# Query projection moved from token-by-token matmuls to the feature stage's block products, its RMS factor applied as the exponential's scale, sample attention in the third pass

## The chip, the core and the metric

The kernel runs on one core of a Trainium2 chip. The metric is the device time of one execution in microseconds (us); lower is better. The engines are called PE (TensorE, matmuls), DVE (VectorE), ACT (ScalarE), POOL (GpSimd) and SP (SyncE, which issues nearly all DMAs).

## The reference, cut to what matters

One layer for a prompt of 2048 tokens and 32 sample tokens (2080 together), model width 1024. The change touches the query path:

```python
h = rms_norm(x, norm_g) * (1.0 + scale[:, None, :]) + shift[:, None, :]
proj = h @ w_in
(q, k, v, za, qi, ki, wi, u, bg, cg, zb, ga, gb) = jnp.split(proj, ...)
q = partial_rope(rms_norm(q.reshape(B, T, 8, 128), q_norm_g), pos)   # 16 + 16 rotated dims of 128
k = partial_rope(rms_norm(k.reshape(B, T, 2, 128), k_norm_g), pos)
...
s = einsum('bqhgd,bqkhd->bqhgk', qg, kg) * (128 ** -0.5)
p = softmax(where(valid, s, -inf))                                   # over the 256 keys that an indexer picks
```

The RMS norm of a query is one factor for each token and head, times `q_norm_g` for each dimension. A rotation does not change the sum of squares, so the factor can be taken at any point before the softmax.

## The kernel before, in words

All large matmuls are fp32 split in two parts, so that a product is three matmuls (high by high, high by low, low by high). The program has four stages.

**Token stage** (`tok_steps`). The tokens come in two halves of 1040 columns (8 tiles of 128; the second half has a ninth tile of 32). `mk_h` transposes the normalised input, keeps it split in `hhi` and `hlo` and stores it in `h_d`. `chunk` then computes, for one tile of tokens and one piece of weights from the list `TOK`, 8 x 3 matmuls with tokens on the output's partitions (L759 to L761) into one of five accumulators `pm`. The pieces are `i0`, `i1` (indexer), `k`, `q0` to `q3` (256 columns each) and `v`. For `k` and `q` the norm's squares are ACT's (L726), the power is POOL's (L183), and scaling (L733) and rotation (L716 to L720) are DVE's; queries go to `q_d`, a row for each token. In the second half, `block_sums` (L670) forms differences of quarters of `h_d` for the next stage and stores them in `t_d`: 12 pieces, each of two loads of 352 (or 336) KB into the `x` buffers, of which there are four, four DVE operations and two stores. They are inserted among the last 50 steps, one for every three chunks.

**Feature stage** (`unit_steps`). The other projections are kept by feature: features on the output's partitions, tokens on the columns. They are computed by a scheme of seven half-size products in place of eight. A unit is two blocks of 128 features; each of its seven products is 12 matmuls for each of three chunks of 352, 352 and 336 columns (L991 to L993, in `mm`). `PASSES` deals the seven products over three passes: three, two and two. The first pass stores its results in `u_d`; the second ends the first half of the tokens, the third the second half (`fin`, which starts with an add of accumulator and stored part, L1053). `b_piece` loads and splits the token side of the products: from `h_d` or `t_d` to `ev` buffers (seven), ACT makes the high part `bh` and DVE the low part `bl` (L187). The first unit needs nine such pieces. There are 28 units in `PAIRS`.

Beside the units, `weave` mixes in the index selection of the blocks of queries (`index_steps`: scores by two matmuls each, L242 and L243, ReLU on ACT, accumulation on DVE, L246 and L248, then a bisection), nine blocks in the first pass, three in the second, three in the third. The attention of the 32 sample tokens (`sample_steps`) stands in the first pass, behind block 13.

**Attention** (`attention`). For each of 16 blocks of 128 queries, `prep` loads queries of a group of four heads, transposes them on PE (L1302) and splits them. `qk` computes scores (L1327 to L1329), adds a mask while it takes the row maximum (L1338), and applies `Exp` on ACT with the constant scale 128 ** -0.5 (L1342). `pv` multiplies with the values (L1363, L1371 to L1375).

**Output stage** (`outputs`): three more projections by the same scheme of seven products.

The order on each engine is set by a scheduler that places instructions by its own estimate of time, within the program's dependences; memory of a pool that has ended is given to the next one, so that the feature stage's `ev` buffers lie where the token stage's `x` buffers were, and its `wr` buffers where the token weights were.

## Time and profile before

| | |
|---|---|
| median of 3 runs | 2857.86 us (2855.92 to 2862.1) |
| profiled execution | 2855.3 us |
| its span, first to last instruction | 2853.4 us |
| PE busy | 2768.8 us, 97% |
| DVE / ACT / POOL busy | 2211.7 / 1486.7 / 971.3 us |
| token stage, last token matmul | starts at 460.96 us |
| first block product | starts at 465.63 us |
| first `u_d` load (second pass) | 1080.5 us |
| moved by DMA | 557.19 MB |

In the profile's lists a row of a group gives line, engine, operation, names and shape, the count, then busy time and mean duration, then the idle time of the engine just before them and what ended it. A row of time gives start, duration, engine, line, operation, and in brackets idle time before it. A row of waits gives who waited for whom, the sum, the number of times and the longest. "To landing" is the time from a DMA's issue to its last byte. A row of stretches gives busy time and number of instructions for each engine.

### The profile page before, as it was taken

The numbers are of one execution on the slowest core, as the hardware profiler recorded it, in microseconds if no ns is written. First come the engines' busy times: TensorE is split into PE (matmuls) and PEld (weight loads), VectorE is DVE, ScalarE is ACT, GpSimd is POOL, SyncE is SP. The second block draws the span as 40 slices with busy tenths as digits, with TensorE's granted clock in tenths as the row PEclk, the third lists the DMA queues.
The fourth block names the chain that finished last, engine by engine and source line by source line (L and its number), as shares of the span: only waits on it lengthen the run. The fifth ranks groups of instructions, "written<-read, shape, count | busy, mean of one in ns | idle before, by whom it ended". The sixth has DMA issues, their size and how long they took to land. (4 is left out here: it accounts for less than half of the span.)

```text
span 2853.4 us, 53721 instructions
## 1 busy us (share of the span) xinstructions
PE 2768.8 (97%) x18926; PEld 2674.1 (94%) x18926; DVE 2211.7 (78%) x4981; ACT 1486.7 (52%) x2861; POOL 971.3 (34%) x1440
## 2 busy tenths in 40 slices
PE   8999998999999999999999999999999999999998
PEld 6999998999999998999999999889999989999998
DVE  6666576767764778999998777878877768987988
ACT  4434334665545665655554433665655555454453
POOL 3324224545554532322323221576544430010100
PEclk9999999999999999999999999999999999999999
DMA  7425567544554546555576676576555359996785
GB/s 290 165 88 190 170 209 246 191 146 165 167 182 148 168 153 223 184 185 175 181 249 212 204 238 184 146 179 185 149 156 160 113 179 339 279 296 217 249 297 157
DMA packets 462097, 557.19 MB, mean 195 GB/s; under 512 B 171441, under 2 KB 353145, under 8 KB 460793
## 3 DMA queue, kind: packets, MB, share of 16 engines
q1 hardware_dynamic: 452952, 537.33, 59.1%
q0 software_dynamic: 4160, 12.06, 1.2%
q10 hardware_dynamic: 4704, 4.26, 0.4%
q8 instruction: 151, 2.47, 0.4%
q14 instruction: 130, 1.06, 0.1%
HBM read 369.17 MB, written 190.66 MB: 196 GB/s over the span
## 5 line engine op out<-in xcount | busy, mean ns | idle before, releaser
L991 PE MATMUL pm<-bh,wo 128*128 128x352 f32 (+1 forms) x2352 | 755.1, 323 | 6.5 <-ACT ev L1003 4.4
L992 PE MATMUL pm<-bl,wo 128*128 128x352 f32 (+1 forms) x2352 | 756.0, 322 | 0.0
L993 PE MATMUL pm<-bh,wo 128*128 128x352 f32 (+1 forms) x2352 | 754.2, 322 | 0.0
L991 PEld LDWEIGHTS pm<-bh,wo 128*128 128x128 f32 x2352 | 443.3, 189 | 15.1 <-ACT ev L1003 5.7
L992 PEld LDWEIGHTS pm<-bl,wo 128*128 128x128 f32 x2352 | 443.9, 189 | 4.8
L993 PEld LDWEIGHTS pm<-bh,wo 128*128 128x128 f32 x2352 | 442.3, 188 | 4.2 <-issue 0.2
L187 POOL TENSOR_TENSOR wo<-wr,wo 128x512 fp32r<-128x512 f32 x140 | 204.8, 1463 | 597.6 <-ACT wo L186 582.7
L759 PE MATMUL pm<-wh,hhi 128*128 128x256 f32 (+4 forms) x1088 | 307.9, 285 | 5.7 <-DVE sm L733 5.5
L760 PE MATMUL pm<-wl,hhi 128*128 128x256 f32 (+4 forms) x1088 | 307.2, 283 | 2.9 <-DVE wl L187 1.7
L761 PE MATMUL pm<-wh,hlo 128*128 128x256 f32 (+4 forms) x1088 | 305.0, 283 | 0.0
L248 DVE SCALAR_TENSOR_TENSOR sc<-pi,wi,sc 128x512 f32<-128x512 f32 (+3 forms) x287 | 192.2, 670 | 56.7 <-ACT pi L244 53.7
L186 ACT CAST th<-pt 128x512 fp32r<-128x512 f32 (+1 forms) x288 | 155.1, 561 | 137.7 <-PE pt L1363 131.1
L244 ACT ACTIVATE pi<-pi 128x512 f32<-128x512 f32 (+3 forms) x328 | 164.8, 516 | 113.1 <-PE pi L243 112.2
L1459 ACT CAST wh<-rw 128x1024 fp32r<-128x1024 f32 x128 | 134.3, 1052 | 166.0 <-PE ps L1634 81.2
L1633 PE MATMUL ps<-xh,wh 128*128 128x384 f32 (+1 forms) x672 | 214.2, 321 | 2.4 <-ACT wh L1459 0.9
L1634 PE MATMUL ps<-xl,wh 128*128 128x384 f32 (+1 forms) x672 | 214.4, 320 | 0.0
L187 DVE TENSOR_TENSOR tl<-pt,th 128x512 fp32r<-128x512 f32 (+1 forms) x288 | 183.9, 655 | 38.5 <-ACT th L186 37.3
L1635 PE MATMUL ps<-xh,wl 128*128 128x384 f32 (+1 forms) x672 | 211.7, 320 | 0.5 <-DVE wl L1460 0.5
L759 PEld LDWEIGHTS pm<-wh,hhi 128*128 128x128 f32 (+1 forms) x1088 | 198.9, 183 | 8.2 <-issue 3.5
L760 PEld LDWEIGHTS pm<-wl,hhi 128*128 128x128 f32 (+1 forms) x1088 | 199.2, 183 | 4.7 <-POOL wl L187 1.5
L761 PEld LDWEIGHTS pm<-wh,hlo 128*128 128x128 f32 (+1 forms) x1088 | 198.4, 183 | 1.0 <-DVE hlo L187 0.2
L1460 DVE TENSOR_TENSOR wl<-rw,wh 128x1024 fp32r<-128x1024 f32 x128 | 155.3, 1220 | 47.9 <-ACT wh L1459 47.7
(313 smaller groups left out, 7168.6 us busy)
## 6 DMA issues: line engine op xcount, KB each, us to landing
u<-u_d SPq DMA_DIRECT2D x112, 520.0 KB, 4.5
wr<-in_w_f_dram SPq DMA_DIRECT2D x84, 512.0 KB, 3.9
rw<-o_d SPq DMA_DIRECT2D x72, 512.0 KB, 6.8
u_d<-ev SPq DMA_DIRECT2D x168, 176.0 KB, 2.5
rw<-in_w_q_dram SPq DMA_DIRECT2D x56, 512.0 KB, 7.3
wr<-in_w_t_dram SPq DMA_DIRECT2D x32, 512.0 KB, 4.4
xa_d<-a SPq DMA_DIRECT2D x64, 256.0 KB, 3.1
s_d<-ws SPq DMA_DIRECT2D x56, 256.0 KB, 2.8
```

Of the source, the lines that this page charges most:

```text
L187: (eng or V).tensor_tensor(lo, src, hi.bitcast(F32), ALU.subtract)
L244: S.activation(pi[:n, :w], pi[:n, :w], AF.Relu)
L248: V.scalar_tensor_tensor(sc[:n, o:o + w], pi[:n, :w], wi[:n, b, h:h + 1], sc[:n, o:o + w], ALU.mult, ALU.add)
L759: T.matmul(pm[:n, :ncol], a, hi[:, kt, :ncol], start=(kt == 0), stop=False)
L760: T.matmul(pm[:n, :ncol], a, lo[:, kt, :ncol], start=False, stop=False)
L761: T.matmul(pm[:n, :ncol], b_, hi[:, kt, :ncol], start=False, stop=(kt == KT - 1))
L991: T.matmul(ps[:, :tb], wh[:, kt, :], bh[:, kt, :tb], start=(first and kt == 0), stop=False, **more)
L992: T.matmul(ps[:, :tb], wh[:, kt, :], bl[:, kt, :tb], start=False, stop=False, **more)
L993: T.matmul(ps[:, :tb], wl[:, kt, :], bh[:, kt, :tb], start=False, stop=(kt == 3), **more)
L1633: T.matmul(ps[:, :tb], wh[:, kt, wc], xh[:, kt, :tb], start=(first and kt == 0), stop=False, **more)
L1634: T.matmul(ps[:, :tb], wh[:, kt, wc], xl[:, kt, :tb], start=False, stop=False, **more)
L1635: T.matmul(ps[:, :tb], wl[:, kt, wc], xh[:, kt, :tb], start=False, stop=(kt == 3), **more)
```

## The change

- The query leaves `TOK` (four of eight pieces) and joins `PAIRS` as four units at the head of each pass, 32 units in all. Its weight columns are dealt (`QCOL`) so that a block of 128 features holds 16 dimensions of each of the eight heads; blocks 0 and 1 hold the 32 rotated dimensions.
- `query` takes the place of `fin` for these units: it adds the stored part, squares (ACT) and sums the squares over the eight blocks, multiplies with `q_norm_g`, rotates blocks 0 and 1 with tables that are loaded for it (two products on POOL, four operations on DVE for each chunk), and stores. A block of 128 features is stored by eight DMAs of 16 rows, so that `q_d` becomes [head, dimension, token].
- `factors` sums the squares over a head by ten small matmuls for each half, adds the epsilon and takes the power -0.5; the result, which holds the factor 128 ** -0.5 as well, goes to `r_d`, a row of 8 for each token.
- In attention the queries are loaded with the dimension on the partitions, so that their transposes go; the split reads the loaded tile. The factor of token and head is the scale of `Exp`, and of its bias. The sample attention likewise.
- The block sums of the second half start at step 15 of the token steps, one for every two chunks.
- The sample attention stands behind the third pass's index blocks.

Its core:

```diff
-PAIRS = []
+PAIRS = [("q", 2 * _u, 7 * KT + 2 * _u) for _u in range(KT // 2)]
-TOK += [(f"q{_i}", [(CQ + 256 * _i, 256)]) for _i in range(4)] + [("v", [(CV, 256)])]
+TOK += [("v", [(CV, 256)])]
+QCOL = [CQ + 128 * _h + 16 * _t + _i for _t in range(KT) for _h in range(8) for _i in range(16)]
...
-    q_d = dp.tile([NTOK, 1024], F32, name="q_d", tag="q_d")
+    q_d = dp.tile([8, P, NTOK], F32, name="q_d", tag="q_d")
+    r_d = dp.tile([NTOK, 8], F32, name="r_d", tag="r_d")
...
             def softmax():
-                V.tensor_scalar(w[:, 3:4], w[:, 2:3], -SCALE, None, ALU.mult)
-                S.activation(st["s"], st["s"], AF.Exp, bias=w[:, 3:4], scale=SCALE, accum_out=w[:, 4:5])
+                V.tensor_scalar(w[:, 3:4], w[:, 2:3], w[:, 6:7], -1.0, ALU.mult, ALU.mult)
+                S.activation(st["s"], st["s"], AF.Exp, bias=w[:, 3:4], scale=w[:, 6:7], accum_out=w[:, 4:5])
...
-                at = len(steps) - 50
+                at = 15
                 for j in range(12):
                     ch, kt = j // 4, j % 4
                     steps.insert(at, (0.0, lambda ch=ch, kt=kt: sums_load(ch, kt)))
                     steps.insert(at + 3, (0.1, lambda ch=ch, kt=kt: block_sums(ch, kt)))
-                    at += 5
+                    at += 4
...
+            if kind == "q":
+                query(ct, f, hf, ch, uu, ps, second)
+                return
...
+        def query(ct, f, hf, ch, uu, ps, second):
+            ...
+            V.tensor_tensor(u, u, ps[:, :tb], ALU.add)
+            ...
+            if ct == 0 and not second:
+                S.activation(sg, u, AF.Square)
+            else:
+                S.activation(sq, u, AF.Square)
+                V.tensor_tensor(sg, sg, sq, ALU.add)
+            S.mul(u, u, vecs[:, 88 + ct + f:89 + ct + f])
+            if ct == 0:
+                ...
+                G.tensor_tensor(x, a, sin, ALU.mult)
+                G.tensor_tensor(y, b, sin, ALU.mult)
+                V.tensor_tensor(a, a, cos, ALU.mult)
+                V.tensor_tensor(b, b, cos, ALU.mult)
+                V.tensor_tensor(a, a, y, ALU.subtract)
+                V.tensor_tensor(b, b, x, ALU.add)
+                if last:
+                    q_store(1 - f, t0, cvy["uu"])
+            if last:
+                q_store(ct + f, t0, uu)
+                if ct == KT - 2 and second:
+                    soon.append(lambda sg=cvy["ss"]: factors(sg, t0))
+        def q_store(t, t0, uu):
+            for h in range(8):
+                store(q_d[h, 16 * t:16 * t + 16, t0:t0 + HT], uu[16 * h:16 * h + 16, :HT])
+        def factors(sg, t0):
+            pq = pst.tile([P, 512], F32, name=nm("pq"), tag="pt")
+            for j in range(10):
+                T.matmul(pq[:104, 8 * j:8 * j + 8], sg[:, 104 * j:104 * j + 104], heads, start=True, stop=True)
+            ...
+            store(r_d[t0:t0 + HT, :].rearrange("(j p) h -> p j h", p=104), ss[:104].rearrange("p (j h) -> p j h", h=8))
...
             for b in blocks:
                 side += index_steps(env, b, False)
-                if b == 13:
-                    side += sample
+            if ps == 2:
+                side += sample
...
-                            load(q, q_d[r0:r0 + P, 512 * g:512 * g + 512])
+                            load(q.rearrange("p (h t) -> p h t", h=4), q_d[4 * g:4 * g + 4, :, r0:r0 + P].rearrange("h d t -> d h t"))
-                        pt = ptile().rearrange("p (h q) -> p h q", h=4)
-                        for h in range(4):
-                            T.transpose(pt[:, h, :], q[:, h * P:(h + 1) * P], ident)
-                        split(qh, ql, pt)
+                        split(qh, ql, q.rearrange("p (h q) -> p h q", h=4))
...
-                        V.tensor_scalar(sc[:, 16 + i:17 + i], sc[:, c1:c1 + 1], -SCALE, None, ALU.mult)
-                        S.activation(sm[:, :L], sm[:, :L], AF.Exp, bias=sc[:, 16 + i:17 + i], scale=SCALE, accum_out=sc[:, 18 + i:19 + i])
+                        r = st["r"][:, 2 * pr + i:2 * pr + i + 1]
+                        V.tensor_scalar(sc[:, 16 + i:17 + i], sc[:, c1:c1 + 1], r, -1.0, ALU.mult, ALU.mult)
+                        S.activation(sm[:, :L], sm[:, :L], AF.Exp, bias=sc[:, 16 + i:17 + i], scale=r, accum_out=sc[:, 18 + i:19 + i])
```

**How the order moves at the change from token to feature stage.** On PE, before, from the last token matmul on: `qd` to `pt` are transposes for the index scores of the sample block, `pi` index scores, `pm` with `bh` a block product.

```order
L761 MATMUL pm_6721<-wh_6153,hlo 32x256
L233 MATMUL pt_6989<-ident,qd_6983 128x32 x4
L242 MATMUL pi_6997<-kiS,qh_6987 32x352
L242 MATMUL pi_7007<-kiS,qh_6987 32x352
L991 MATMUL pm_6959<-bh_6775,wo_6771 128x352
```

Now, at the same place (line numbers are those of the changed kernel: L762 token, L237 transpose, L246 and L247 index score, L988 block product):

```order
L762 MATMUL pm_3856<-wh_3202,hlo 32x256
L237 MATMUL pt_4124<-ident,qd_4118 128x32 x4
L246 MATMUL pi_4132<-kiS,qh_4122 32x352
...
L237 MATMUL pt_4248<-ident,qd_4243 128x32 x4
L246 MATMUL pi_4274<-kiS,qh_4246 32x352
...
L237 MATMUL pt_4726<-ident,qd_4721 128x128 x4
L246 MATMUL pi_4734<-kiT,qh_4724 128x512
...
L247 MATMUL pi_4824<-kiT,ql_4725 128x512
L988 MATMUL pm_4094<-bh_3910,wo_3906 128x352
```

Between the last token matmul and the first block product stand now 48 index matmuls of 352 columns, 16 of 512 and 12 transposes, where two index matmuls and four transposes stood.

On SP, before, from the last block sum's load to the first operand of the feature stage (`x` and `t_d` the block sums, `q_d` the queries' stores, `ev` the operand):

```order
L661 DMA x_6115<-h_d 128x2x336
L776 DMA q_d<-sm_6143 128x256
L776 DMA q_d<-sm_6196 128x256
L672 DMA t_d<-x_6114 256x1x336
L776 DMA q_d<-sm_6243 128x256
L672 DMA t_d<-x_6115 256x1x336
L226 DMA qd_7108<-qi_d 32x4x64
...
L776 DMA q_d<-sm_6451 128x256
L977 DMA ev_6777<-h_d 128x352
```

Now (L662 and L673 the block sums, L925 feature weights, L974 the operand):

```order
L673 DMA t_d<-x_3647 256x1x336
L673 DMA t_d<-x_3648 256x1x336
L662 DMA x_3718<-h_d 128x2x336
L662 DMA x_3719<-h_d 128x2x336
L230 DMA qd_5710<-qi_d 128x4x64
L231 DMA qd_5710<-qi_d 128x4x64
L673 DMA t_d<-x_3718 256x1x336
L673 DMA t_d<-x_3719 256x1x336
L925 DMA wr_3902<-in_w_f_dram 128x1024
L925 DMA wr_3904<-in_w_f_dram 128x1024
L974 DMA ev_3912<-h_d 128x352
```

Of the 24 stores of the block sums, the last fourteen have no store of a token tile's keys between them any more; before, stores of queries stood between them to the end.

On DVE, after the last key tile's rotation (L721), what follows in the changed kernel (L671 the block sums, L209 an index key):

```order
L721 TENSOR_TENSOR sm_3591<-sm_3594 32x2x16
L209 TENSOR_TENSOR kiS<-pt_3606,kh_3608 64x128
L671 TENSOR_TENSOR x_3156<-x_3156 128x352
L671 TENSOR_TENSOR x_3156<-x_3157,x_3156 128x352
L671 TENSOR_TENSOR x_3157<-x_3157,x_3156 128x352
L671 TENSOR_TENSOR x_3157<-x_3157 128x352
L671 TENSOR_TENSOR x_3268<-x_3268 128x352
```

The piece that begins here is the sixth of twelve; before, the last piece was followed by the norm and rotation of six more query tiles. In the third pass, the sample attention's last matmul stands 144 block products ahead of attention's first score.

More of the change, by code (lines that the diff above doesn't have):

```diff
@@ L410, in prep @@
                     load(st["m"][h * NS:(h + 1) * NS, :], ms_d)
-                q = env.small()
-                load(q[:NS], q_d[SEQ:, 512 * g:512 * g + 512])
-                pt = env.pst.tile([P, 512], F32, name=nm("pt"), tag="pt")
+                load(st["q"].rearrange("p (h t) -> p h t", h=4), q_d[4 * g:4 * g + 4, :, SEQ:].rearrange("h d t -> d h t"))
+                w = st["w"] = env.ip.tile([P, 64], F32, name=nm("w"), tag="w", bufs=2)
                 for h in range(4):
-                    T.transpose(pt[:, h * NS:(h + 1) * NS], q[:NS, h * P:(h + 1) * P], ident[:NS, :NS])
-                S.copy(st["q"], pt[:, :P])
-                st["w"] = env.ip.tile([P, 64], F32, name=nm("w"), tag="w", bufs=2)
+                    load(w[h * NS:(h + 1) * NS, 6:7], r_d[SEQ:, 4 * g + h:4 * g + h + 1])
             def logits(c):
@@ L1396, in attention @@
                     qst = sp.tile([P, SEQ], F32, name=nm("s"), tag="low")[:, :1024]
-                    load(qst, q_d[order[0] * P:order[0] * P + P, :])
+                    load(qst.rearrange("p (h t) -> p h t", h=8), q_d[:, :, order[0] * P:order[0] * P + P].rearrange("h d t -> d h t"))
                     vst = ahead(v_d)
@@ L1821, in _consts @@
     table = np.concatenate([table, np.zeros((17 * P - NTOK, 48), np.float32)]).reshape(17, P, 48).transpose(1, 0, 2).reshape(P, 17 * 48)
-    return {"rope": table, "ident": np.eye(P, dtype=np.float32), "rows": rows}
+    turns = np.stack([np.tile(t.T, (8, 1)) for t in cols[:2]]).astype(np.float32)
+    heads = np.kron(np.eye(8), np.ones((16, 1)))
+    return {"rope": table, "turns": turns, "ident": np.concatenate([np.eye(P), heads], axis=1).astype(np.float32), "rows": rows}
 def _chunks(w):
-    cols = np.concatenate([np.asarray(w)[:, c:c + D] for c in FCOL], axis=1)
-    return cols.reshape(KT, P, 7 * KT, P).transpose(2, 1, 0, 3).reshape(7 * KT, P, KT * P)
+    cols = np.concatenate([np.asarray(w)[:, c:c + D] for c in FCOL] + [np.asarray(w)[:, QCOL]], axis=1)
+    return cols.reshape(KT, P, 8 * KT, P).transpose(2, 1, 0, 3).reshape(8 * KT, P, KT * P)
 def _wide(w):
```

66 lines of the change are left out of this document (48 added, 18 removed).

## The prediction

> **What bounds the kernel now.** I read the page's busy totals first, then the stretches of the span, then who waits for whom on TensorE. The totals say that one engine is nearly full:
>
> ```profile
> span 2853.4 us, 53721 instructions
> PE 2768.8 (97%) x18926; PEld 2674.1 (94%) x18926; DVE 2211.7 (78%) x4981; ACT 1486.7 (52%) x2861; POOL 971.3 (34%) x1440
> ```
>
> TensorE is idle for 2853.4 - 2768.8 = 85 us in all, so a change is worth what it takes from TensorE's stream, less any new hole in it. The stretches show both, and what stands behind TensorE in each stage (columns: length, then busy time and count by engine, granted clock, DMA share, GB/s):
>
> ```profile
> core 0: us, PE busy (x) PEld busy (x) DVE busy (x) ACT busy (x) POOL busy (x), PEclk, DMA share, GB/s
> 150.00:200.00 50.00, 50.00 (x444) 50.00 (x443) 32.09 (x158) 17.01 (x78) 13.70 (x20) 1.00 0.31 103
> 350.00:400.00 50.00, 46.89 (x406) 45.93 (x405) 37.26 (x161) 16.81 (x78) 13.30 (x21) 1.00 0.72 228
> 1250.00:1300.00 50.00, 49.51 (x306) 48.45 (x305) 48.87 (x105) 27.34 (x53) 14.13 (x18) 1.00 0.51 174
> 1400.00:1440.00 40.00, 40.00 (x254) 40.00 (x253) 35.35 (x83) 22.36 (x47) 11.87 (x13) 1.00 0.64 215
> 1800.00:1850.00 50.00, 46.76 (x333) 43.35 (x332) 39.68 (x133) 28.73 (x73) 33.37 (x98) 0.94 0.66 151
> 1900.00:1950.00 50.00, 44.51 (x311) 40.79 (x310) 36.09 (x94) 27.86 (x57) 33.60 (x87) 0.97 0.69 187
> 2350.00:2400.00 50.00, 47.97 (x272) 46.68 (x271) 39.51 (x61) 27.07 (x32) 7.42 (x14) 1.00 0.97 345
> ```
>
> At 150 the token stage runs without a hole: 444 matmuls of 256 columns, less one or two cut by the edges, in 50 us, so one starts every 0.113 us. At 1400 only block products run: 254 in 40 us, one every 0.1575 us for 352 or 336 columns. These spacings, not the durations of 0.28 and 0.32 us, are what a matmul costs, since the next starts before the last ends. At 350, in the second half of the tokens, DMA is 0.72 full at 228 GB/s, so full would be 317. At 1250, in the second pass, VectorE is as full as TensorE. At 1800 to 1950 attention's first blocks leave TensorE idle for some 3 to 5 us in 50.
>
> **The sum.** *Query projection out of the token stage.* Four pieces, 17 tiles, 8 contraction steps, 3 products: 1632 matmuls, x 0.113 = -184.4 us. *Four more units in the feature stage.* 7 products, 3 column chunks, 4 steps, 3 matmuls each: 1008 x 0.1575 = +158.8. Net -25.6. TensorE was full in both stretches, so this is path.
>
> On these two spacings the Trainium skill (TensorE: Matmul & The Clock Gate, Back-to-back issue gap) has a sustained roofline of 81 ns at 128 columns and 131 ns at 512. An estimate between those points is 98 and 109 ns, and the net would be -50 us; the rows are longer, by more at 350 columns, and they decide.
>
> *Attention's query transposes.* The list of TensorE in order of time, one group of four:
>
> ```profile
> 1789.58 0.28 PE L1372 MATMUL po<-tl,vhi 128*128 128x256 f32 x1
> 1789.70 0.29 PE L1373 MATMUL po<-th,vlo 128*128 128x256 f32 x1
> 1789.83 0.60 PE L1302 MATMUL pt<-ident,in 128*128 128x128 f32 x4
> 1790.18 0.36 PE L1371 MATMUL po<-th,vhi 128*128 128x256 f32 x1
> 1790.38 0.35 PE L1372 MATMUL po<-tl,vhi 128*128 128x256 f32 x1
> 1790.57 0.28 PE L1373 MATMUL po<-th,vlo 128*128 128x256 f32 x1
> 1790.69 0.28 PE L1371 MATMUL po<-th,vhi 128*128 128x256 f32 x1
> ```
>
> Four take 0.35 us and the next two start 0.20 and 0.19 apart where 0.12 is usual: 0.50 a group. 16 blocks have two: 32 x 0.50 = 16. Half of the blocks lie in the stretches at 1800 to 1950, where TensorE has holes that such a group may merely fill; I take -12, bounds -16 and 0. The split behind them stays, from SBUF instead of PSUM. The loads get runs of 512 bytes instead of 2 KB; before, they held TensorE for
>
> ```profile
> PE pt L1302 <- DMA in<-q_d: 2.5, 2, 1.3
> ```
>
> in all, and from now on the split waits for them, with TensorE's work on the block before as cover.
>
> *Waits that go with the norm.* TensorE's waits in the token stage are mostly for the norm that frees an accumulator:
>
> ```profile
> PE pm L759 <- DVE sm L733: 5.5, 6, 1.4
> ```
>
> Four of its five users go: -4, bounds -5.5 and 0. VectorE's own norm, rotation and weight splits for the queries go too; in that stage they lay beside TensorE.
>
> *The RMS factors.* Two groups of ten small matmuls, f32 as the transposes are: at a transpose's 0.35 / 4 about 0.9 us a group, or 1.25 with the slower matmuls after it: +2; bounds 0 and +4 if each group waits 1 us for VectorE's sum. The factor as scale replaces a constant and costs nothing; 16 small loads share SP with the mask loads.
>
> *The change of stage, and who is late next.* The block sums (L670) have to be done before the feature stage: their four `x` buffers lie where its `ev` buffers come. Before, their work and landings were:
>
> ```profile
> L670 DVE TENSOR_TENSOR x<-x x24: 487/510/526, 323.6 to 432.2; 128x352 f32<-128x352 f32 x16, 128x336 f32<-128x336 f32 x8
> DMA x<-h_d: 13.5, 12
> x<-h_d SPq DMA_DIRECT2D x16, 352.0 KB, 3.7
> t_d<-x SPq DMA_DIRECT2D x16, 352.0 KB, 2.7
> 405.88 0.61 SPq L661 DMA_DIRECT2D x<-h_d  x1
> L248 DVE SCALAR_TENSOR_TENSOR sc<-pi,wi,sc 128x512 f32<-128x512 f32 (+3 forms) x287 | 192.2, 670 | 56.7 <-ACT pi L244 53.7
> L186 ACT CAST bh<-ev 128x352 fp32r<-128x352 f32 (+1 forms) x84 | 37.4, 477 | 18.4 <-DMA ev<-h_d 12.3 <-DMA ev<-t_d 5.5 <-DVE y L1045 0.3
> ev<-h_d SPq DMA_DIRECT2D x8, 176.0 KB, 4.3
> ```
>
> Twelve pieces ran from 323.6 to 432.2, hidden under queries until 461. Now they must run beside the last 22 chunks of index, key and value, 22 x 24 x 0.113 = 60 us of TensorE. Two pieces fit in the buffers. A cycle is two loads to issue (1.2), 3.7 to land, four operations of 0.51, a store to issue (0.6), 2.7 to land, 1.1 of wait as in the 12 waits of the row, and, an estimate, 1.5 for VectorE's queue, two or three operations: 12.8 us for two pieces, 6.4 each. DMA gives no less: 16.6 MB of sums, 4.2 of keys and values, 1.9 of weights and index is 22.7 MB, 72 us at 317 GB/s, 6.0 a piece. I take 6.5: 78 us, then 4.3 for the first `ev`, 0.5 cast, 0.5 difference (as long as a block sum's), 1.2 to issue two: the first block product 84.5 us after the first load, 24.5 us behind the last token matmul. Index scores pulled into the hole (the order above) fill 48 x 0.16 + 16 x 0.24, by columns, and 12 transposes x 0.09: 12.6; VectorE needs about that gap for them anyway (32 scores of some 0.6, the row's mean for 512 columns being 0.67, and three pieces of 2.04 are 25 us). That leaves 12 idle. The nine operand pieces behind, 6.2 MB, want 19.6 us at 317 GB/s where TensorE wants 9 x 12 x 0.1575 = 17: 3 more. Before, the same place idled:
>
> ```profile
> 464.85 0.61 PE L242 MATMUL pi<-kiS,qh 128*32 128x352 f32 x2 [3.25 <-ACT qh L186]
> 465.63 0.66 PE L991 MATMUL pm<-bh,wo 128*128 128x352 f32 x1 [0.17 <-ACT wo L186]
> 477.14 0.34 PE L242 MATMUL pi<-kiS,qh 128*32 128x352 f32 x1 [2.65 <-DVE sc L248]
> 478.05 0.34 PE L242 MATMUL pi<-kiS,qh 128*32 128x352 f32 x1 [0.41 <-DVE sc L246]
> 478.73 0.50 PE L242 MATMUL pi<-kiS,qh 128*32 128x352 f32 x1 [0.17 <-DVE sc L248]
> ```
>
> 6.6 us. So +12 + 3 - 6.6, about +9.
>
> *Query units in passes two and three.* A unit lasts 6 x 12 x 0.1575 = 11.3 us without index work. VectorE's part per step is an add, and a square's add of the same size; rotation adds four operations per chunk in one unit:
>
> ```profile
> L1053 DVE TENSOR_TENSOR u<-u,pm 128x352 f32<-128x352 f32 (+1 forms) x240 | 121.0, 506 | 24.3 <-PE pm L993 23.5
> L940 POOL TENSOR_TENSOR ws<-wr 128x512 f32<-128x512 f32 x28 | 37.1, 1325 | 93.6 <-DMA wr<-in_w_f_dram 55.1 <-DMA u_d<-ev 19.0 <-issue 13.3
> u<-u_d SPq DMA_DIRECT2D x112, 520.0 KB, 4.5
> L1014 SPq DMA_DIRECT2D u<-u_d x112: 319/320/1540, 1080.5 to 1764.6; - x112
> ```
>
> Per pass 24 + 21 + 12 operations of 0.506 are 29 us in 45 us of TensorE time, less than VectorE's 48.87 of 50 around it: covered by TensorE. The rotation's subtraction waits for two products on POOL, 0.9 us each by columns, beside two of VectorE's own; behind it in VectorE's queue stand the adds that free accumulators, and five accumulators give 4 x 12 x 0.1575 = 7.6 us of slack. Instead of one store a tile there are eight of 16 rows; the sixteen at the end of the first unit hold back, on SP, the load of the third unit's `u` by about 16 x 0.32 = 5 us plus landing; the second unit's 11.3 us and the slack cover that and the load's 4.5: +2 for what they don't, bounds 0 and +29 if VectorE's part is not covered.
>
> *Sample attention* keeps its work, less eight transposes (under 1 us, left out). In the third pass it ends 144 block-product matmuls, 23 us, before attention's first scores: no term, and if that cover were gone, attention would wait for it by no more than one group's last steps.
>
> Sum: -25.6 - 12 - 4 + 2 + 9 + 2 = -28.6. The profiled execution took 2855.3 (span 2853.4 and 1.9 around it), so 2826.7; the median of the runs is 2857.86, 2.6 above it, so 2829.3 there.
>
> **Rivals.** *No hole at the change of stage.* With the shortest landings, 3.3 and 2.7, and no queueing, the cycle is 1.2 + 3.3 + 2.04 + 0.6 + 2.7 = 9.8, 4.9 a piece, 59 us, and the sums end with the tokens:
>
> ```profile
> DMA to landing us min/median/max: 3.3/3.7/6.1
> DMA to landing us min/median/max: 2.7/2.7/3.8
> ```
>
> Then the +9 goes, and with all 16 us of the transposes it is 2816. Against it: the loads of the whole stretch then ask for more than 317 GB/s. The Trainium skill (DMA: Bandwidth & Descriptors, Anatomy of one DMA) has about 2 us plus bytes over 436 GB/s, 2.8 us as an estimate for these loads, on this rival's side; the trace's 3.3 at best differs.
>
> *VectorE is the bound in the second pass.* At 48.87 of 50 it has no room if the index selection's operations crowd the new ones; each accumulator is then freed late, and 29 us come onto the path: 2858, no change. For it speaks that stretch, against it that the selection's total stays while the pass grows.
>
> *DMA holds the feature stage back, and it is slower.* Before, from 300 to 461, it moved
>
> ```profile
> DMA packets 26861, 33.34 MB, mean 207 GB/s; under 512 B 3231, under 2 KB 25690, under 8 KB 26842
> ```
>
> If 207 GB/s is what these short packets get, the 30 MB up to the ninth operand piece (22.7, 6.2 and 1 of weights) take 145 us against 60 + 17 of TensorE: 68 us late, less 12.6 filled and the 6.6 of before, +49 in place of +9: 2869. It decides below 224 GB/s, where the whole gain of 37.6 us outside this term is used up. Against it: 228 at a share of 0.72, and 345 in the stretch at 2350.
>
> **How the numbers follow.** Forecast 0.62, no hole 0.14, VectorE 0.13, DMA 0.11. The forecast's own terms reach from 2812 to 2843. The range 2810 to 2860 takes in the first three and leaves out the fourth and some of the tails. Within 0.2% (5.7 us, about what a measurement of this kernel can tell from no change) is 2852 to 2864: 0.13, mostly the third case. Slower: 0.09. Faster: 0.78.
>
> **What would show it.** The last token matmul starts near 273 (461 less 184 and 4); between it and the first block product lie 20 to 30 us with index scores in them; the block sums follow one another at 6 to 7 us; the feature stage is some 160 us longer; no waits for the query in attention, which is 10 to 16 us shorter. Wrong if the hole passes 50 us, or if the second pass has more than 5 us of new idle TensorE time.

## The result, and the profile after

The changed kernel takes 2874.12 us (median of 6 runs, 2868.78 to 2879.44), the kernel before 2857.7 on the same chip. The ratio is 1.0051, 95% interval 1.0029 to 1.0073: slower by 0.5%, where the forecast was 2829 and faster. Medians and ratios below are of undisturbed executions; two executions of the experiments' kernels, of 3538 and 15314 us, are left out as slow. The profiled execution took 2868.78 us, its span is 2867.0. From the page of the changed kernel, the busy totals:

```profile
span 2867.0 us, 51829 instructions
PE 2749.5 (96%) x18206; PEld 2642.5 (92%) x18206; DVE 2193.7 (77%) x4549; ACT 1508.4 (53%) x2719; POOL 1049.3 (37%) x1430
```

TensorE has 19 us less to do, and is idle for 2867.0 - 2749.5 = 117.5 us where it was 85. The stretches show where:

```profile
core 0: us, PE busy (x) PEld busy (x) DVE busy (x) ACT busy (x) POOL busy (x), PEclk, DMA share, GB/s
250.00:300.00 50.00, 33.81 (x230) 25.36 (x229) 24.72 (x61) 11.20 (x31) 2.29 (x6) 0.78 0.78 245
300.00:350.00 50.00, 34.26 (x121) 21.68 (x121) 46.32 (x87) 37.80 (x79) 25.85 (x21) 0.77 0.77 247
1000.00:1050.00 50.00, 44.20 (x245) 40.99 (x244) 41.40 (x94) 37.28 (x76) 18.56 (x18) 0.93 0.68 200
1250.00:1300.00 50.00, 50.00 (x318) 49.98 (x317) 34.63 (x58) 19.04 (x36) 13.17 (x9) 1.00 0.59 184
```

Between 250 and 350 TensorE ran 351 instructions; a full stretch of 50 us holds 318 of the feature stage's or 444 of the token stage's. The second pass (1250) is full, and VectorE has 15 us free in it. TensorE in order of time, at the change of stage:

```profile
270.99 0.28 PE L762 MATMUL pm<-wh,hlo 128*32 128x256 f32 x1
271.20 0.43 PE L237 MATMUL pt<-ident,qd 32*128 32x32 f32 x4
275.88 0.76 PE L246 MATMUL pi<-kiS,qh 128*32 128x352 f32 x2 [4.25 <-DVE kiS L209]
284.17 0.50 PE L247 MATMUL pi<-kiS,ql 128*32 128x352 f32 x1 [7.53 <-DVE ql L191]
...
318.41 0.32 PE L988 MATMUL pm<-bh,wo 128*128 128x352 f32 x1
320.15 0.66 PE L989 MATMUL pm<-bl,wo 128*128 128x352 f32 x1 [0.31 <-DVE bl L191]
```

The last token matmul starts at 270.99, the first block product at 318.4: 47.4 us apart, where it was 465.63 - 460.96 = 4.7. What VectorE and SP's queue do there (first row: duration, then first and last start; the others in order of time; last row of the group of loads):

```profile
L671 DVE TENSOR_TENSOR x<-x x24: 485/522/589, 213.8 to 308.9; 128x352 f32<-128x352 f32 x16, 128x336 f32<-128x336 f32 x8
269.98 1.74 SPq L662 DMA_DIRECT2D x<-h_d  x2
276.32 1.68 SPq L673 DMA_DIRECT2D t_d<-x  x2
278.04 1.30 SPq L662 DMA_DIRECT2D x<-h_d  x2
283.82 1.84 SPq L673 DMA_DIRECT2D t_d<-x  x2
285.71 1.28 SPq L662 DMA_DIRECT2D x<-h_d  x2
DMA to landing us min/median/max: 3.9/4.7/4.9
```

The block sums run from 213.8 to 308.9, and the loads of the twelve pieces start from 207.5 to 302.2: eleven steps of 8.6 us. SP issues the two stores of a piece, and only then the two loads of the next: one piece is in flight, and each cycle is an issue, a landing of 4.7 and VectorE's four sums in a row, with index scores between them on VectorE (stores waited 10.0 us in all behind those, by the list of SP's waits).

The length of attention comes from its first score and the first matmul of the output stage, the two rows of before and then the two of after:

```profile
L1327 PE MATMUL ps<-khi,qh x320: 277/394/796, 1780.4 to 2316.5; 128*128 128x512 f32 x92, 128*128 128x384 f32 x59, 128*128 128x256 f32 x5, 128*128 128x128 f32 x4
L1633 PE MATMUL ps<-xh,wh x672: 283/336/452, 2349.2 to 2790.7; 128*128 128x384 f32 x112, 128*128 128x272 f32 x56
```

```profile
L1392 PE MATMUL ps<-khi,qh x320: 222/394/657, 1808.6 to 2328.1; 128*128 128x512 f32 x91, 128*128 128x384 f32 x60, 128*128 128x256 f32 x5, 128*128 128x128 f32 x4
L1699 PE MATMUL ps<-xh,wh x672: 283/336/445, 2359.8 to 2803.9; 128*128 128x384 f32 x112, 128*128 128x272 f32 x56
```

| part, us | before | after | difference | forecast |
|---|---|---|---|---|
| up to the last token matmul | 461.0 | 271.0 | -190.0 | -188.4 |
| hole to the first block product | 4.7 | 47.4 | +42.7 | +19.8 (24.5 - 4.7) |
| first block product to first score | 1314.8 | 1490.2 | +175.4 | about +152 |
| first score to output stage | 568.8 | 551.2 | -17.6 | -12 |
| output stage | 504.2 | 507.2 | +3.0 | 0 |

The forecast's +152 is 158.8 of block products, +2 and +2 for factors and query units, +3 for operand pieces, less the 12.6 of index scores that the hole was to take out and 2 of idle time before. So two terms are wrong by some 23 us each: the hole, and the feature stage.

### The profile page after: what moved, and what is told of

It reads as the page before. It is cut to its first block, busy times and chain, and to the rows that moved or that the text cites. A ratio compares the mean times of both kernels' runs of the same rounds, so it can differ in the third digit from the quotient of the medians.

```text
span 2867.0 us, 51829 instructions
## 1 busy us (share of the span) xinstructions
PE 2749.5 (96%) x18206; PEld 2642.5 (92%) x18206; DVE 2193.7 (77%) x4549; ACT 1508.4 (53%) x2719; POOL 1049.3 (37%) x1430
## 5 line engine op out<-in xcount | busy, mean ns | idle before, releaser
L988 PE MATMUL pm<-bh,wo 128*128 128x352 f32 (+1 forms) x2688 | 867.0, 324 | 13.1 <-DVE u L1087 8.4
L989 PE MATMUL pm<-bl,wo 128*128 128x352 f32 (+1 forms) x2688 | 866.3, 322 | 2.2 <-DVE bl L191 2.1
L990 PE MATMUL pm<-bh,wo 128*128 128x352 f32 (+1 forms) x2688 | 864.0, 323 | 0.4 <-POOL wo L191 0.4
L988 PEld LDWEIGHTS pm<-bh,wo 128*128 128x128 f32 x2688 | 508.1, 189 | 21.6 <-DVE u L1087 10.1
L989 PEld LDWEIGHTS pm<-bl,wo 128*128 128x128 f32 x2688 | 509.2, 189 | 9.4 <-DVE bl L191 3.5
L990 PEld LDWEIGHTS pm<-bh,wo 128*128 128x128 f32 x2688 | 507.9, 189 | 4.0 <-POOL wo L191 0.8
L1408 ACT ACTIVATE s<-s,sc,rts 128x640 f32<-128x640 f32 (+15 forms) x128 | 166.0, 1298 | 49.6 <-DVE sc L1407 43.5
L1780 POOL DMA_DIRECT2D out_dram<-om x60 | 31.7, 534 | 389.9 <-DVE om L1778 389.9
L190 ACT CAST wo<-wr 128x512 fp32r<-128x512 f32 x160 | 98.3, 616 | 144.3 <-PE pm L989 114.4
L315 ACT ACTIVATE low<-sc,w 32x1056 f32<-32x1056 f32 (+14 forms) x105 | 136.6, 1301 | 62.7 <-DVE w L320 61.8
L1053 DVE TENSOR_TENSOR u<-u,pm 128x352 f32<-128x352 f32 (+1 forms) x240 | 122.2, 510 | 56.6 <-PE pm L990 54.9
L1437 PE MATMUL po<-th,vhi 128*128 128x256 f32 x544 | 158.9, 292 | 5.3 <-ACT th L190 3.0
```

The source lines that it names most:

```text
L190: S.copy(hi, src)
L988: T.matmul(ps[:, :tb], wh[:, kt, :], bh[:, kt, :tb], start=(first and kt == 0), stop=False, **more)
L989: T.matmul(ps[:, :tb], wh[:, kt, :], bl[:, kt, :tb], start=False, stop=False, **more)
L990: T.matmul(ps[:, :tb], wl[:, kt, :], bh[:, kt, :tb], start=False, stop=(kt == 3), **more)
L1408: S.activation(sm[:, :L], sm[:, :L], AF.Exp, bias=sc[:, 16 + i:17 + i], scale=r, accum_out=sc[:, 18 + i:19 + i])
```

## The experiments

Theory A: the hole is the chain of the block sums, one piece in flight because of the order on SP's queue. Theory B: the transfers themselves set it. Theory C: the feature stage's start is slow by itself, since VectorE is crowded. Theory D: the eight stores of a query tile hold passes two and three back. Twelve kernels; ratios are to the kernel before, in the same set of runs:

| kernel | median us | ratio, 95% interval | hole us | first block product to first score |
|---|---|---|---|---|
| loads one piece ahead | 2864.54 | 1.0021 (1.0007 to 1.0035) | 21.9 | 1504.6 |
| no block sums | 2827.98 | 0.9901 (0.9880 to 0.9923) | 4.7 | 1491.6 |
| index woven in later | 2875.66 | 1.0067 (1.0046 to 1.0089) | 47.2 | 1492.7 |
| sums started earlier | 2851.53 | 0.9981 (0.9968 to 0.9993) | 11.0 | 1498.1 |
| earlier and ahead | 2850.72 | 0.9960 (0.9942 to 0.9977) | 11.3 | 1498.1 |
| one store a query tile | 2876.71 | 1.0055 (1.0041 to 1.0070) | 49.4 | 1491.8 |
| index held back | 2884.58 | 1.0097 (1.0072 to 1.0121) | 42.3 | 1507.9 |
| earlier, ahead, one store | 2850.08 | 0.9963 (0.9951 to 0.9976) | 7.2 | 1496.6 |
| plain query units | 2865.72 | 1.0020 (1.0009 to 1.0031) | 49.3 | 1480.4 |
| constant scale in Exp | 2873.42 | 1.0057 (1.0041 to 1.0072) | 47.7 | 1494.6 |
| square sums on POOL | 2849.06 | 0.9968 (0.9955 to 0.9980) | 8.9 | 1496.1 |
| half of the splits on POOL | 2850.50 | 0.9979 (0.9966 to 0.9991) | 10.3 | 1495.9 |

**Loads one piece ahead.**

```diff
+                steps.insert(at, (0.0, lambda: sums_load(0, 0)))
                 for j in range(12):
-                    steps.insert(at, (0.0, lambda ch=ch, kt=kt: sums_load(ch, kt)))
-                    steps.insert(at + 3, (0.1, lambda ch=ch, kt=kt: block_sums(ch, kt)))
+                    if j < 11:
+                        steps.insert(at + 1, (0.0, lambda j=j: sums_load((j + 1) // 4, (j + 1) % 4)))
+                    steps.insert(at + 3, (0.1, lambda j=j: block_sums(j // 4, j % 4)))
```

> The changed kernel with the loads of each block-sum piece issued before the sums of the piece before it, so that two pieces are in flight; nothing else is different. Theory A (queue order: in the changed kernel the loads of a piece stand on SP's queue behind the stores of the piece before, so only one piece is in flight and pieces follow each other every 8.3 to 8.6 us): the pieces come 6.4 to 7 us apart, the last sum ends near 290 instead of 309, the first block product starts near 300 instead of 318, and the time falls by 12 to 20 us, to 2854 to 2862. Theory B (the transfers set the pace, at 170 to 297 GB/s in that stretch): the pieces stay over 8 us apart and the time stays within 4 us of 2874.

Its sums, its first block product, and two of its stretches:

```profile
L671 DVE TENSOR_TENSOR x<-x x24: 485/522/536, 212.6 to 288.3; 128x352 f32<-128x352 f32 x16, 128x336 f32<-128x336 f32 x8
L989 PE MATMUL pm<-bh,wo x2688: 311/321/726, 296.5 to 1799.8; 128*128 128x352 f32 x132, 128*128 128x336 f32 x60
```

```profile
250.00:260.00 10.00, 10.00 (x89) 10.00 (x89) 7.79 (x39) 1.30 (x7) 2.38 (x5) 1.00 0.98 308
260.00:270.00 10.00, 10.00 (x90) 10.00 (x89) 3.61 (x7) 1.56 (x5) 0.42 (x2) 1.00 1.02 330
```

The loads of a piece now follow those of the piece before by 6.3 us (209.1 to 278.4 in eleven steps), the last sum starts at 288.3, the hole is 21.9: A, and near what the forecast had taken for the change itself (6.5 and 24.5). B does not explain the 8.6 us, but it is the next limit: in these 20 us DMA is full, at 308 to 330 GB/s. Only some 9 us of the 25 from the hole reach the end, where 12 to 20 were expected: the token stage ends 3.7 us later and the feature stage is 14 longer. Less index work was done in the hole (48 instructions of TensorE for 77) and the first unit is still slow (21 products of a line in its first 42 us); how the 14 divide between the two was not measured.

**No block sums** (the sums are left out, and eleven of twelve pieces of their loads; the stores of all twelve stay).

```diff
+            if (ch, kt) != (0, 0):
+                return
...
-                tc.keep_in_program_order(V.tensor_tensor(o, p, q, ALU.subtract))
+            x1, x2 = halved[0, 0]
```

> The changed kernel with the block sums left out: the two buffers of the first piece are loaded once and stored for all twelve pieces, so the twelve stores to the DRAM array stay, and eleven of twelve pieces of loads and all of VectorE's subtractions go (the outputs of the feature stage are then not the reference's). Theory A (the chain of load, subtraction and store sets the hole of 47.5 us): the first block product comes 5 to 15 us behind the last token matmul and the time falls by 30 to 40 us, to 2834 to 2844. Theory B (transfers): half of the traffic stays, so that a hole of some 25 us stays, 2850. Theory C (the start of the feature stage is slow by itself, since VectorE is full with operand splits, index scores and the sample block's bisection in the first 40 us): the hole goes, but in the first 42 us after the first block product there are still less than 100 of them on a third of the lines, and the time falls by less than 30.

```profile
L986 PE MATMUL pm<-bh,wo x2688: 311/321/726, 276.3 to 1767.1; 128*128 128x352 f32 x132, 128*128 128x336 f32 x60
```

The first block product comes 4.7 us behind the last token matmul (at 271.7), as before the change, and the time falls by 46 us, more than expected, to 1% below the kernel before. In its first 42 us the first unit runs 57 products on L986; it was 53 before the change and is 24 after it. (The 100 that the expectation set as its mark could not be reached: 42 us hold 42 / (3 x 0.1575) = 89.) So the slow first unit, too, comes from the sums, which keep the `ev` buffers from it until 309; C, as a cost that would be there without the sums, falls. Yet its feature stage is as long as after the change, 1491.6, now with all index work in it: 176.8 over before, and 14 over the 158.8 + 4 of the forecast. That rest is not the block sums'.

**Index woven in later, and index held back.** First by the order of the program alone, then with an order kept on TensorE as well, which was meant to put the transposes of the first two index blocks behind the first unit's matmuls.

```diff
+            if ps == 0:
+                weave(main[:9], [], FAST)
+                main = main[9:]
             weave(main, side, FAST)
```

> The changed kernel with the index work of the first pass woven in only after the first unit of the feature stage; all the work is done. Theory A (the hole alone is the cost, and the index scores that run in it are a gain of about 12 us): the hole stays near 47 us and is empty, and the time rises by 5 to 12 us, to 2879 to 2886. Theory C (the index scores and the bisection crowd the operand splits on VectorE after the hole): the block products run at full rate soon after the first, 180 or more on one of the three lines in the first 42 us instead of 24, which gains some 13 us; with the 12 us of index scores that move out of the hole the time is 2868 to 2876.

```diff
+                if b > 14:
+                    tc.keep_in_program_order(m)
...
+            if n == 0:
+                tc.keep_in_program_order(m)
...
```

> The changed kernel with the index scores of the first two index blocks of the feature stage kept, on TensorE, behind the matmuls of the first unit; all the work is done. Theory C (index scores and bisection crowd the operand splits on VectorE and so slow the first unit): in the first 42 us behind the first block product there are 50 or more block products on one of the three lines instead of 24; the hole of 47 us stays and is empty, so its 12.6 us of index scores come back later, and the time is 2868 to 2880. Rival (the operand pieces come that slowly by DMA, or their casts and splits alone take that long): 30 or less, and the time rises by 8 to 14 us, to 2882 to 2888.

The first edit tells nothing: the scheduler pulled the scores into the hole all the same (77 instructions in it, as after the change, and 24 products in the first 42 us), and the 180 of its expectation was out of reach, like the 100 above. In the second the hole is empty of index scores and the time rises by 10.5 us by the medians (13 by the ratios), about the 12.6 of index scores that it held; that part of the forecast is borne out. But the order held only in part. The first unit has nine groups of twelve matmuls, and the scores start behind the fifth of them:

```profile
334.30 0.48 PE L248 MATMUL pi<-kiS,qh 128*32 128x352 f32 x2
```

They then take TensorE until 347.5, inside the 42 us that are counted. So the 32 products on a line, up from 24 and between the 30 and 50 of the expectation, do not show how the first unit would run without index scores, and this run does not decide how large their part is. The trace of the changed kernel shows the engine that sets it: VectorE is busy for 41.39 of these 42 us, and TensorE's idle time in them ends at index scores that wait for VectorE, 11.9 us, of which these are the longest two, and hardly at block products (1.0 us):

```profile
PE pi L246 <- DVE sc L252: 6.2, 4, 2.0
PE pi L247 <- DVE w L316: 3.5, 1, 3.5
```

What came onto VectorE in these 42 us are the splits of the operands. The 36 of the first unit, before the change and then after it:

```profile
L187 DVE TENSOR_TENSOR bl<-ev,bh x36: 484/523/1608, 447.6 to 494.7; 128x352 fp32r<-128x352 f32 x24, 128x336 fp32r<-128x336 f32 x12
L191 DVE TENSOR_TENSOR bl<-ev,bh x36: 486/506/1614, 319.6 to 360.4; 128x352 fp32r<-128x352 f32 x24, 128x336 fp32r<-128x336 f32 x12
```

Before, 15 of them were done ahead of the first block product at 465.63, and the last started 29 us behind it; after, none is done ahead, and the last starts 42 us behind it. Without the sums 15 are done ahead again. In both kernels, a split that meets a POOL operation takes up to 1.6 us instead of 0.5 (see the last section), so that is not what changed.

**Sums started earlier**, one for every three chunks; then **both edits**.

```diff
-                at = 15
+                at = 3
...
-                    at += 4
+                    at += 5
```

> The changed kernel with the block sums started at step 3 instead of 15 of the second half's token steps, one for every three chunks instead of two; still one piece in flight. Theory A (queue order): the pieces stay 8 us or more apart, but begin some 30 us earlier and end near the last token matmul (270 to 285), the first block product starts at 280 to 295, and the time falls by 20 to 35 us, to 2839 to 2854. Theory B (transfers): the earlier pieces hold back the stores and loads of the normalised input, the token stage ends 10 us or more later, and the time falls by less than 15.

> The changed kernel with both edits to the block sums: started at step 3 of the second half's token steps, one for every three chunks, and the loads of a piece issued before the sums of the piece before it. If the two costs are a late start and one piece in flight, the sums end before the last token matmul and the hole closes as it did without the sums: first block product within 10 us of the last token matmul, 2836 to 2846. If DMA is the limit once two pieces are in flight (its share was 0.98 to 1.02 from 240 to 270 us with the loads ahead), the transfers of the token stage itself come late, the token stage ends 8 us or more later than 271, and the time is no better than with the early start alone, 2848 to 2856.

Of the kernel with the early start alone, its sums, its first block product and one stretch:

```profile
L671 DVE TENSOR_TENSOR x<-x x24: 490/518/915, 179.5 to 276.8; 128x352 f32<-128x352 f32 x16, 128x336 f32<-128x336 f32 x8
L988 PE MATMUL pm<-bh,wo x2688: 311/321/726, 289.6 to 1786.4; 128*128 128x352 f32 x128, 128*128 128x336 f32 x64
220.00:230.00 10.00, 5.57 (x30) 4.41 (x29) 9.31 (x24) 4.72 (x9) 2.99 (x6) 0.87 0.75 244
```

The pieces still come 8.5 us apart (loads from 175.9 to 269.4 in eleven steps), but the chain starts 34 us earlier and lies beside token matmuls: 23 us gained, and the kernel is now 0.2% faster than before the change. Here the pace no longer tells how many pieces are in flight, since a place every three chunks, 72 x 0.113 = 8.1 us, could give it by itself. The price is in the stretch at 220, where TensorE waits for the split of the key's weights, late behind the sums' traffic: the last token matmul starts at 278.6 instead of 271. With the loads ahead as well the pieces come no faster (8.4 us), the token stage ends at 281.2, the hole is no smaller, and the ratios of the two overlap: the second expectation's other case, in which the token stage pays.

**One store for a query tile.** The features of a block are dealt by dimension and then head, so that a block's 128 rows lie together in an array [dimension, head, token].

```diff
...
-            for h in range(8):
-                store(q_d[h, 16 * t:16 * t + 16, t0:t0 + HT], uu[16 * h:16 * h + 16, :HT])
+            store(q_d[16 * t:16 * t + 16].rearrange("i h t -> (i h) t")[:, t0:t0 + HT], uu[:, :HT])
```

> The changed kernel with the dimensions and heads of a block of query features dealt the other way round, so that a block is stored by one DMA of 128 rows instead of eight of 16 rows; the array is [dimension, head, token] and attention loads it with the dimension on the partitions as before. Theory D (the eight stores hold back the next unit's loads on SP and its buffers, so that the first query units of passes two and three keep TensorE waiting for VectorE's adds, 8.4 us before matmuls and 10.1 before weight loads): the waits on that add fall to under 4 us each and the time falls by 6 to 12 us. Rival (the waits are those of the stored parts' own loads, or of VectorE's and ScalarE's work in these units, whatever the store's form): the waits stay over 7 and 8 us, and the time stays within 3 us of 2874.

> The changed kernel with the early start of the block sums, their loads one piece ahead, and the query's store as one DMA. If the three effects add up, the time is 6 to 12 us below the kernel with the first two alone: 2828 to 2846, faster than the kernel before the change by 0.4 to 1.0%. If the store's form costs nothing, it is that kernel's time within 3 us.

The waits of TensorE's matmuls for the query's add, after the change and then with one store:

```profile
PE pm L988 <- DVE u L1087: 8.4, 4, 2.6
```

```profile
PE pm L988 <- DVE u L1087: 4.2, 4, 2.1
```

These waits are halved, to neither of the two values expected, and the feature stage stays as long (1491.8), since other waits came up in their place (TensorE's idle time in passes two and three is in the rows of the next experiment). D falls: nothing was gained. Joined with both edits to the sums it is as fast as those alone (ratios 0.9963 and 0.9960).

**Plain query units** (squares, gain, rotation and its loads left out, factors constant) and **constant scale** (the factor left out of the exponential).

```diff
             V.tensor_tensor(u, u, ps[:, :tb], ALU.add)
-            if ct == 0 and not second and ch == 0:
...
-                    q_store(1 - f, t0, cvy["uu"])
             if last:
                 q_store(ct + f, t0, uu)
```

> The changed kernel with the query units reduced to the add of accumulator and stored part and the store: squares, their sums, the multiplication with the norm's gain, the rotation and its table loads are left out, and the factors are made constant (queries and attention are then not the reference's). If VectorE's, ScalarE's and POOL's part of the query units is what the feature stage pays beyond its matmuls (14 us more than the sum had, of which 5 are idle TensorE time in passes two and three), the time falls by 6 to 14 us, to 2860 to 2868. If that part lies beside TensorE, as the forecast had it with 2 us, it falls by 0 to 4 us, to 2870 to 2874, and the excess is not the query's processing.

```diff
-                        V.tensor_scalar(sc[:, 16 + i:17 + i], sc[:, c1:c1 + 1], r, -1.0, ALU.mult, ALU.mult)
-                        S.activation(sm[:, :L], sm[:, :L], AF.Exp, bias=sc[:, 16 + i:17 + i], scale=r, accum_out=sc[:, 18 + i:19 + i])
+                        V.tensor_scalar(sc[:, 16 + i:17 + i], sc[:, c1:c1 + 1], -SCALE, None, ALU.mult)
+                        S.activation(sm[:, :L], sm[:, :L], AF.Exp, bias=sc[:, 16 + i:17 + i], scale=SCALE, accum_out=sc[:, 18 + i:19 + i])
```

> The changed kernel with the constant scale of the kernel before in attention's exponential and its bias, instead of the factor of token and head, which is loaded but not used (the softmax is then not the reference's). If the scale read from memory makes each exponential longer, its mean falls from 1298 ns back to about 1206 ns, the kernel before's; on the forecast's view that lies beside TensorE and the time stays within 4 us of 2874. If the mean stays near 1298, the longer exponentials come from something else, such as when they run.

Without the query's processing the kernel takes 0.3%, 9 us, less (1.0020 against 1.0051), and the feature stage is 9.8 shorter: that is most of the 14 us. Passes two and three, from the first load of `u_d` to the first score, before, after, with one store, and with plain query units:

```profile
1080.50:1780.37 699.87, 693.82 (x4342) 685.54 (x4341) 613.13 (x1386) 348.14 (x693) 187.75 (x193) 1.00 0.63 203
1008.60:1808.56 799.96, 786.02 (x4930) 776.24 (x4931) 623.15 (x1369) 362.58 (x732) 241.66 (x203) 0.99 0.66 208
1009.30:1813.20 803.90, 788.94 (x4933) 777.50 (x4932) 622.58 (x1370) 362.30 (x732) 236.60 (x203) 0.99 0.65 207
1012.60:1803.97 791.37, 783.60 (x4931) 775.70 (x4931) 590.35 (x1302) 322.86 (x636) 225.38 (x191) 1.00 0.66 207
```

TensorE idles there for 6.1, 13.9, 15.0 and 7.8 us: most of what the processing costs is new idle time. The constant scale changes the time by nothing that can be told.

**Two further edits** to the kernel with early sums, loads ahead and one store: the query's sums of squares on POOL, and half of the first unit's splits on POOL.

```diff
-                V.tensor_tensor(sg, sg, sq, ALU.add)
+                G.tensor_tensor(sg, sg, sq, ALU.add)
```

> The kernel with early block sums, loads ahead and one store (2850, 0.37% below the kernel before), and now the sums of the query's squares on POOL instead of VectorE, all work done. The plain query units gained 0.3%: if VectorE's queue is where the query's processing costs, taking 84 of its adds gives a third or so of that, 2 to 4 us, 2846 to 2848. If it costs on POOL and ScalarE as well (rotation products, squares), POOL's adds of some 0.9 us come late, the rotation's products behind them, and the time stays or rises by up to 4 us.

```diff
-                split(hi[:, kt, :tb], lo[:, kt, :tb], r[:, :tb])
+                split(hi[:, kt, :tb], lo[:, kt, :tb], r[:, :tb], eng=G if kt % 2 and k in (0, 1, 3) else V)
```

> The same kernel with early block sums, loads ahead and one store, and now half of the low parts of the first unit's 36 operand rows on POOL instead of VectorE, all work done. If VectorE's queue of splits sets the slow start of the first unit (35 block products on one line in its first 42 us, against 53 in the kernel before), there are 45 or more, and the time falls by 3 to 6 us, to 2844 to 2847. If the two engines hinder each other (VectorE's split took 0.95 us while POOL worked and 0.5 while it did not), or DMA sets the start, there are 40 or less and the time stays within 3 us of 2850 or rises.

Neither gains. With half of the splits on POOL the first unit runs 43 products on a line in its first 42 us instead of 35, between the two values expected, and POOL is now the full engine there (busy for 40.89 of the 42 us). The time stays within 3 us, so the first unit's start is better and something else is later; what, stays open. All versions with the early start lie at 2849 to 2852 us, 0.2 to 0.4% below the kernel before; none reaches the 2828 without sums.

## Why the prediction was wrong

- **The path by TensorE's spacing: right.** Token stage -190.0 for -188.4, the last token matmul at 271 where 273 was said. The net of token and block products was worth having: without the sums the changed kernel takes 2828. That this is the 2829 of the whole forecast is luck, since that kernel leaves work out, has no hole where the forecast had 24.5, and pays 14 us more in the feature stage.
- **Attention: right in kind, larger.** -17.6 for -12; all of the transposes' 16 us counted, and the holes of the first blocks did not take any: TensorE idles for 20.6 us in attention before and 20.1 after.
- **The change of stage: the failed step is "Two pieces fit in the buffers."** They do, but the program puts a piece's loads behind the stores of the piece before, as the order on SP's queue that stands ahead of the prediction already shows, and SP issued them in that order. The forecast halved a cycle that could not be halved. Its own terms one after the other, 1.2 + 3.7 + 2.04 and 1.2 for two stores, give 8.1 us a piece and a hole of 44; measured were 8.6 and 47.4, in place of 6.5 and 24.5, with landings of 4.7 where 3.7 was taken. With the loads ahead it was 6.3 and 21.9. The limit that the forecast named, the hole under 50 us, was nearly reached.
- **The first unit behind the hole: mis-sized.** "3 more" for nine operand pieces was read from DMA and TensorE alone. All 36 splits now came behind the first block product, together with index scores and the sample block's bisection, and VectorE was busy for 46.32 of 50 us at 300. The feature stage is as long as without the sums (1490.2 and 1491.6) although 12.6 us of index scores were already done in the hole: 11 us where 3 was said, 8 more. TensorE's idle time shows as much: 39.1 us against 31.1 without the sums.
- **Query units: mis-sized.** +2 was taken from bounds of 0 and +29; leaving their processing out gave 9. The forecast's reason was the stores; their form made no difference. Its sign of being wrong, more than 5 us of new idle time in the second pass, was nearly reached: there TensorE idles for 8.6 us after 4.1, and passes two and three together have 8 more.
- **Factor as scale, "costs nothing": right for the time, wrong for the engine**, see below.
- **The rivals.** The rival without a hole leaned on 2.8 us for a load; the section of the Trainium skill that the prediction cites for it (DMA: Bandwidth & Descriptors, Anatomy of one DMA) fits its formula to DMAs that GpSimd issues, and SP's loads here took 3.3 us at best before the change and 3.9 after it. VectorE did not become the bound of the second pass (34.63 of 50 us at 1250). The case of DMA held the right end for another reason: at 270 to 310 it moved 229 GB/s, not because it could do no more, but because one piece at a time asked for no more.

The miss of 42 us is then 23 of hole, 8 of first unit, 14 of the feature stage's own (9 of it the query's processing, 5 unsettled), 3 of output stage, less 5.6 in attention and 1.6 in the token stage; that is 41. The small terms are no finer than the profiles agree: in kernels whose edits do not touch the stage, the feature stage took 1490 to 1495 us, attention 551 to 555 and the output stage 505 to 509. The move of the sample attention to the third pass, a part of the change, was not tested by itself.

## What to carry to other kernels

How many pieces were in flight here was the smaller of two numbers: what the buffers held, and how many pieces' loads stood on the queue ahead of the first store that waits for a result; read the second off the queue's list before halving a cycle. When work that covered a serial chain goes, start the chain earlier by the cover's length first: that one number gave 23 us here, the deeper pipeline 9. Both together gained 0.91% by the ratios, after 0.70% and 0.30%, but the intervals of the early start with and without the deeper pipeline overlap, and the trace shows no smaller hole; whether the two add up is not settled.

## What the runs showed of the hardware

**An exponential with a scale from memory is 93 ns longer, the shortest and the longest alike.** The groups of before, of after, and with the constant scale (min/median/max):

```profile
L1342 ACT ACTIVATE s<-s,sc x128: 386/1210/2014, 1784.8 to 2319.9; 128x640 f32<-128x640 f32 x8, 128x128 f32<-128x128 f32 x8, 128x768 f32<-128x768 f32 x8, 128x256 f32<-128x256 f32 x8
```

```profile
L1408 ACT ACTIVATE s<-s,sc,rts x128: 479/1298/2107, 1815.7 to 2331.1; 128x640 f32<-128x640 f32 x8, 128x128 f32<-128x128 f32 x8, 128x768 f32<-128x768 f32 x8, 128x256 f32<-128x256 f32 x8
```

```profile
L1408 ACT ACTIVATE s<-s,sc x128: 387/1208/2017, 1821.3 to 2335.6; 128x640 f32<-128x640 f32 x8, 128x128 f32<-128x128 f32 x8, 128x768 f32<-128x768 f32 x8, 128x256 f32<-128x256 f32 x8
```

479 - 386 = 93 at the short end, 2107 - 2014 = 93 at the long one. The Trainium skill (ScalarE: Activation LUTs, What ACT_TABLE_LOAD costs) has about 93 ns for each such operand; the trace agrees.

**A split on VectorE beside POOL takes three times as long; an index accumulation takes no longer.** The splits of the kernel with the index held back, from 314.8 to 322.2 while POOL works almost without a pause, and from 342.9 to 348 while it stands still (min/median/max, first and last start), and one of POOL's operations of the first stretch:

```profile
L191 DVE TENSOR_TENSOR bl<-ev,bh x6: 1270/1590/1596, 314.9 to 322.1; 128x352 fp32r<-128x352 f32 x6
L191 DVE TENSOR_TENSOR bl<-ev,bh x6: 502/503/510, 342.7 to 347.4; 128x352 fp32r<-128x352 f32 x6
318.75 1.55 POOL L939 TENSOR_TENSOR ws<-wr,ws 128x512 f32<-128x512 f32 x1
```

A split takes 0.50 us alone and 1.59 beside POOL, as long as the POOL operation next to it: in the first stretch the two engines go on one for one. (The 0.95 us in an expectation above is a mean over six such splits and six without POOL.) An accumulation of index scores, with one of its two large operands in TensorE's accumulator memory, takes 0.73 us without POOL and beside it; in the changed kernel, where POOL stands still from 328.80 to 332.58 (two rows of VectorE, one of POOL):

```profile
330.74 0.73 DVE L252 SCALAR_TENSOR_TENSOR sc<-pi,wi,sc 128x512 f32<-128x512 f32 x1
334.48 0.73 DVE L252 SCALAR_TENSOR_TENSOR sc<-pi,wi,sc 128x512 f32<-128x512 f32 x1
334.13 1.56 POOL L191 TENSOR_TENSOR wo<-wr,wo 128x512 fp32r<-128x512 f32 x1
```

The Trainium skill (SBUF — State Buffer, SBUF: two separate sides) has an exclusive lock on a port pair between GpSimd and a VectorE operation with two inputs in SBUF, which these splits have; the trace agrees, with 1.59 us for the splits and an unchanged 0.73 for the accumulations, and no run here took the lock itself apart.

**The granted clock follows the work, down and up.** In the held kernel, with no matmul from 280 to 310:

```profile
280.00:290.00 10.00, 0.00 (x0) 0.00 (x0) 2.03 (x4) 0.00 (x0) 0.00 (x0) 0.50 0.79 246
310.00:320.00 10.00, 3.93 (x10) 2.65 (x11) 5.13 (x4) 5.39 (x11) 6.66 (x5) 0.50 0.82 286
```

```profile
325.98 0.49 PE L992 MATMUL pm<-bh,wo 128*128 128x352 f32 x1
326.27 0.48 PE L990 MATMUL pm<-bh,wo 128*128 128x336 f32 x1
...
327.14 0.32 PE L991 MATMUL pm<-bl,wo 128*128 128x336 f32 x1
327.30 0.32 PE L992 MATMUL pm<-bh,wo 128*128 128x336 f32 x1
```

The clock is 0.50 in the hole and stays there while the first block products, from 314.88 on, wait one by one for their splits. Even back to back they start 0.29 us apart, and 0.16 apart only from 327, 12 us after the first. Here the hole thus cost somewhat more than its length: each back-to-back product of that stretch lost 0.13 us.
